# A hybrid attention block on one core: the last norm moved behind the first head's sigmoids, operands given out later, one more item split ahead, one output block reordered

## The chip, the cores and the metric

The kernel runs on one core of one Trainium2 chip. The metric is the device time of one execution in microseconds (us); the time of a kernel is the median of several executions.

## The reference

512 tokens and 16 meta tokens in front of them (528 positions) with 1024 features pass a layer norm and one wide projection. Two attention branches read it, their gated outputs are merged, projected once more, added to the normed input and normed again:

```
h    = layer_norm(concat(meta, x))
proj = h @ w_in                      # 10240 columns: q,k,v,gate of both branches, two merge gates
y_d  = rms_norm((softmax(q1 k1) - lam * softmax(q2 k2)) @ v) * 0.8        # 8 heads, width 128
y_s  = stick_breaking(q, k) @ v                                           # 16 heads, width 64
br_d = (y_d * silu(g_d)) @ w_br_diff ;  br_s = (y_s * silu(g_s)) @ w_br_sb
out  = layer_norm(2**0.25 * h + (sigmoid(m_d + b) * br_d + sigmoid(m_s + b) * br_s) @ w_out)
```

The stick-breaking weights are `sigmoid(z)` times a running product of `sigmoid(-z)`, so this branch needs sigmoids on ScalarE where the first branch needs exponentials, and the rms norm of a softmax head needs a logarithm and an exponential.

## The kernel before

All products run in float32 as three passes (high times high, high times low, low times high). So every weight tile is split before use: ScalarE casts it to `wh` (`hi`, line 153), VectorE subtracts to get `wl` (`lo`, line 158). One such tile of 128 x 512 is an **item**; 212 of them pass through 6 buffers each of `wh` and `wl`. `prep(h)` splits item `h`, and the projections call it for the item four further on (`AHEAD = 4`); it also calls `fetch`, which issues the next weight loads on SyncE's queue, and whatever was put on the list `later` for that many calls of `prep`.

The work has four parts.

- **Start**: layer norm, transposes, the first queries and keys; its order on each engine is as written.
- **Attention**: 16 units, first eight softmax heads ("d"), then eight pairs of stick-breaking heads ("s"). `run` (a loop over the projections of the next unit) hands out the current unit's steps at fixed points of a clock that counts projection work: scores, transposes of the attention weights (`transposed`: copies `ah` on ScalarE at line 625, remainders `al` on VectorE at line 626), products with the values (`d_values`, `s_values`, the latter at lines 774 to 783 into the one bank `av`). In this part the compiler's scheduler decides the final order on each engine, from a simulated time line. A softmax head's norm (`d_norm`: `ms` product at lines 735 and 736, Ln at 738, Exp at 739, VectorE's product at 741 that frees the bank `av`) is handed out 3.0 into the next unit, for the last head (7) 1.0. `s_scores` takes two sigmoids of each score bank (lines 760 and 762), then VectorE's scan (764) and product (765). There are two score banks (`psc`). Line 761 ties every sigmoid behind the newest Exp of a norm, so that ScalarE loads the table of the sigmoids once.
- **Merge and branch products**: order as written. Seven merge gates (`md` 3 to 7, `ms` 0 and 1) are projected while `operands(ydT)` forms the seven operand combinations `gh`, `gl` of the first branch in four parts (lines 850 to 857), given out at 0.3 and then every 7.5. Each branch product is four pairs of column blocks with seven products each (`pair`, line 875; copies of intermediate sums at 880, 882 and 884), a fast scheme that saves one product in eight. The `late` pool that holds `gh`, `gl` and their temporaries lies where the attention's buffers were, so its first writer waits for the last reader of those.
- **Output**: the gated sums are cast to `mh` (line 916) and `ml` (919), `w_out` is split to `wo0h`, `wo0l`, `wo1h`, `wo1l` (lines 936 and 937), and eight groups of 24 products (lines 993 to 995) run over four row blocks and two column halves. In the meantime SyncE loads the residual's parts (`eg`, `eb`, `hr`) and the rest of `w_out`; VectorE forms residual (966, 967), sum (1002), statistics (1005) and the final norm (1015, 1019).

Of the kernel before, what the change touches and what calls it, by code (L numbers as in the profile page):

```python
# [16 lines left out]
P = 128  # L17
D = 1024
KT = D // P
# [24 lines left out]
def hybrid_block_kernel(ctx: ExitStack, tc: tile.TileContext, x, meta, emb_g, emb_b, w_in, b_gate,  # L44
                        diff_lambda, subln_g, w_br_d, w_br_s, w_out, ln_g, ln_b, out):
    nc = tc.nc
    v, s, g, pe = nc.vector, nc.scalar, nc.gpsimd, nc.tensor
# [36 lines left out]
    for n, (kind, i) in enumerate(seq):  # L84
        if kind in ("BD", "BS"):
            w = w_br_d if kind == "BD" else w_br_s
# [21 lines left out]
    raw0 = ypool.tile([P, 4, KT, P], F32, tag="ys", name="raw0")  # L108
    raws, split, sums, later = {}, [], {}, []
    rings = {False: ("raw", 6, []), True: ("rawa", 4, [])}  # L110
    state = {"l": 0, "h": 0, "n": 0}
    pools = {False: wpool}

    def first_load(n):
# [44 lines left out]
        if isinstance(items[h], int):  # L159
            left[items[h]] -= 1  # L160

    AHEAD = 4

    def prep(h):

        state["n"] += 1
# [15 lines left out]
    def follow(ins, other):  # L182
        tc.add_manual_dep(ins, other.name, mybir.DependencyInfo(mybir.DependencyClass.NoSync, mybir.DependencyReason.DATA),
                          reason="order")

    def keep_order(first, engines=ORDERED):

# [249 lines left out]
    def proj_tok(res, kind, i):  # L437
        n = take(kind, i)
        ps = pj.tile([P, 512], F32, tag="pj", name="ps")
        for k in range(KT):  # L440
            if k % 4 == 0:
                prep(n + k // 4 + AHEAD)
            _, wh, wl = split[n + k // 4]
            pe.matmul(ps, wh[:, k % 4, :], hTh[:, k, M:], start=(k == 0), stop=False)  # L444
            pe.matmul(ps, wh[:, k % 4, :], hTl[:, k, M:], start=False, stop=False)  # L445
            pe.matmul(ps, wl[:, k % 4, :], hTh[:, k, M:], start=False, stop=(k == KT - 1))  # L446
            if k < KT - 1:
                yield 0.64
        res.append(ps)

    def proj_pos(res, kind, i):
        n = take(kind, i)
        for c in range(2):
            ps = pj.tile([P, 512], F32, tag="pj", name="ps")
            if n > 4:
                prep(n + c + AHEAD)
            for k in range(KT):
                _, wh, wl = split[n + k // 4]
                for m, (a, b) in enumerate(((wh, hTh), (wh, hTl), (wl, hTh))):
                    pe.matmul(ps[:, :H2], a[:, k % 4, :], b[:, k, ts(c, H2)], start=(k == 0 and m == 0),  # L460
                              stop=(k == KT - 1 and m == 2))
                if k < KT - 1:
                    yield 0.33
            res.append(ps)
            if c == 0:
                yield 0.33
# [34 lines left out]
    with tc.tile_pool(name="att", bufs=1) as ap:  # L501
# [230 lines left out]
        def d_norm(unit, h):  # L732
            av, sq = unit["av"], unit["sq"]
            ms = ptp.tile([P, 512], F32, tag="tp", name="ms")
            pe.matmul(ms, onesm, sq[0], start=True, stop=False)
            pe.matmul(ms, onesm, sq[1], start=False, stop=True)
            r = ap.tile([P, S], F32, tag="sq", name="r")
            s.activation(r, ms, AF.Ln, bias=epsr)
            s.activation(r, r, AF.Exp, scale=-0.5)
            state["exp"] = nc.cur_bb.bb.instructions[-1]  # L740
            v.scalar_tensor_tensor(ydT[:, h, :], av, g08, r, op0=ALU.mult, op1=ALU.mult)


        def s_scores(unit, c):
            K = unit["K"]
            A = unit["A"]
            a = apads[c]
            sg = ap.tile([P, ZW], F32, tag="e0", name="sgm", bufs=2)
            om = ap.tile([P, ZW], F32, tag="e1", name="om", bufs=2)
            for i in reversed(range(NB)):  # L750
                nk, z0 = NKEY[i], ZOFF[i]
                for n, (ps, k0, use, lo) in enumerate(logits(A[c], K[c], i)):
                    if n == 1:
                        yield
                    if k0 + use == nk:
                        w = P if lo is None else use
                        v.tensor_tensor(ps[:, use - w:use], ps[:, use - w:use], with_lo(lo, neg[:, M + P - w:], om[:, ds(z0, w)]),  # L757
                                        op=ALU.add)
                    o = ds(z0 + k0, use)
                    s.activation(om[:, o], ps[:, :use], AF.Sigmoid, scale=-1.0)  # L760
                    follow(nc.cur_bb.bb.instructions[-1], state["exp"])
                    s.activation(sg[:, o], ps[:, :use], AF.Sigmoid)
                rev = om[:, z0:z0 + nk][:, ::-1]
                v.tensor_tensor_scan(rev, rev, rev, 1.0, ALU.mult, ALU.min)  # L764
                v.tensor_tensor(a[:, ds(AOFF[i], nk - 1)], sg[:, ds(z0, nk - 1)], om[:, ds(z0 + 1, nk - 1)],
                                op=ALU.mult)
                yield
# [20 lines left out]
        def spread(gen, t0, dt, count):  # L788
            return [(t0 + dt * m, lambda: next(gen)) for m in range(count)]
# [12 lines left out]
        for u, (kind, n) in enumerate(UNITS):  # L802
            unit = units[u]
            last = u + 1 == len(UNITS)
            proj = [] if last else keys_values(units[u + 1], *UNITS[u + 1])
            if u + 2 < len(UNITS):
                proj.append(stage_q(units[u + 2], *UNITS[u + 2]))
            steps = pending + [(0.6, lambda unit=unit: values(unit, kind))]
            pending = []
            if kind == "d":  # L810
                ta = {}
                steps += spread(d_scores(unit, n), 0.0, TD[0], 10)
                parts = transposed(ta, apads[n % 2], "d")
                steps += [(TD[1] + 0.7 * m, f) for m, f in enumerate(parts)]
                steps.append((TD[2], lambda: d_values(unit, ta)))
                pending = [(3.0 if n < 7 else 1.0, lambda unit=unit, n=n: d_norm(unit, n))]
            else:
                if n == 0:
                    for a in apads:
                        for i in range(NB):  # L820
                            g.memset(a[:, ds(AOFF[i] + NKEY[i] - 1, 1)], 0.0)
                if last:
                    proj += [gate("d", n, ydT), merge_gate(0, 0), merge_gate(0, 1), merge_gate(0, 2), gate("s", n, ysT)]
                else:
                    proj += [gate("d", n, ydT), gate("s", n, ysT)]
                for c in range(2):
                    ta = {}
                    steps += spread(s_scores(unit, c), 4.4 * c + (2.0 if n == 0 and c == 0 else 0.0), 0.85, 5)
                    parts = transposed(ta, apads[c], c)
                    steps += [(7.0 + 6.5 * c + 0.7 * m, f) for m, f in enumerate(parts)]  # L830
                    steps.append((10.5 + 6.5 * c, lambda c=c, ta=ta: s_values(unit, c, n, ta)))
            run(proj, steps)
# [28 lines left out]
    def pair(kind, p, G, t, done):  # L861
# [6 lines left out]
        u, z7, w = c11, c22, c21 = [tmp[:, n, :] for n in range(3)]  # L868

        def product(q, bank, n, start=True):  # L870
            prep(h + q + AHEAD)
            _, wh, wl = split[h + q]
            for k in range(4):
                for m, (a, b) in enumerate(((wh, gh), (wh, gl), (wl, gh))):
                    pe.matmul(bank, a[:, k, :], b[:, n, k, :], start=start and k == 0 and m == 0, stop=k == 3 and m == 2,  # L875
                              skip_group_check=not start)
                yield 0.35
# [22 lines left out]
    G, parts = operands(ydT)  # L900
    early_ms = [gpool.tile([P, S], F32, tag="sg", name="sm1") for j in range(2)]
    run([merge_gate(0, j, MD[j]) for j in range(3, 8)] + [merge_gate(1, j, early_ms[j]) for j in range(2)],
        [(0.3 + 7.5 * i, f) for i, f in enumerate(parts)])
    for p in range(4):
        run([pair("BD", p, G, MD[2 * p:2 * p + 2], lambda m: None)])
    ss = ypool.tile([P, KT, S], F32, tag="yd", name="ss")
# [25 lines left out]
    def split_out(c, k):  # L932
# [5 lines left out]
        left[l] -= 1  # L938
        fetch()

    for p in range(4):
        steps = []
        if p == 3:
            run([merge_gate(1, 7, MS[7])])
            WO = [[hpool.tile([P, KT, 512], F32R, tag=f"hT{x}", name=f"wo0{x}") for x in "hl"]]
            steps = [(0.8 + 1.6 * k, lambda k=k: split_out(0, k)) for k in range(5)]
        run([pair("BS", p, G, MS[2 * p:2 * p + 2], lambda m, p=p: merged(2 * p + m))], steps)
# [36 lines left out]
    for c in range(2):  # L984
        for t in range(NB):
            st, final = sts[t], t == NB - 1
            for o, w in [(0, 256), (256, 256)] if final and c else [(0, 512)]:
                r, hr = ds(o, w), hrs[t][c]
                ps = pj.tile([P, 512], F32, tag="pj", name="pso")[:, :w]
                for n, k in enumerate((0, 1, 2, 3, 4, 5, 7, 6)):  # L990
                    mh, ml = MH[k][:, ts(t, P)], ML[:, k, ts(t, P)]
                    wh, wl = WO[c][0][:, k, r], WO[c][1][:, k, r]
                    pe.matmul(ps, mh, wh, start=(n == 0), stop=False)
                    pe.matmul(ps, mh, wl, start=False, stop=False)
                    pe.matmul(ps, ml, wh, start=False, stop=(n == KT - 1))
                if o == 0:
                    for work in MEANWHILE[NB * c + t]:
                        work()
# [63 lines left out]
```

## Time and profile before

| what | value |
|---|---|
| median of 3 runs | 737.57 us (736.24 to 739.0) |
| the profiled execution | 738.3 us |
| its span, first to last instruction | 736.5 us |
| TensorE busy, share of the span | 721.0 us, 98% |
| VectorE busy | 579.1 us, 79% |
| ScalarE busy | 445.3 us, 60% |
| mean granted TensorE clock | 0.993 |
| DMA | 71.84 MB, 98 GB/s on average |

The profiled execution lies 0.7 us above the median, and 1.8 us of it are outside the span. Line numbers are those of the kernel before; in the changed kernel the same lines stand 6 to 16 further down. "PE" is TensorE's matmul, "ACT" ScalarE, "DVE" VectorE, "POOL" GpSimd, "SPq" SyncE's queue. A matmul's duration is longer than the step from its start to the next one's start, since matmuls are pipelined: what a stall costs is read from the starts.

### The profile page before, as it was taken

Reading aid. Unit: us, or ns where it says so; the run is one execution under the profiler, and the core shown is the slowest. Engines: PE = TensorE matmul, PEld = TensorE weight load, DVE = VectorE, ACT = ScalarE, POOL = GpSimd, SP = SyncE. Lnnn points to the kernel's source line nnn. Section 1 sums busy time; section 2 is a strip of 40 time slices with the busy share of each in tenths; the row PEclk is TensorE's granted clock in tenths of the full one; section 3 lists DMA queues with packets and bytes.
Section 4 is the critical chain, followed back from the end, with each engine's and each line's share of the span. In section 5 each row is a group of like instructions: output and inputs, shape, how many; then the busy total and the mean of one; then the engine's idle time right before and its main releaser. Section 6 shows DMA issues by size and latency. Waiting matters only on the chain.

```text
span 736.5 us, 13070 instructions
## 1 busy us (share of the span) xinstructions
PE 721.0 (98%) x4658; PEld 658.0 (89%) x4658; DVE 579.1 (79%) x1304; ACT 445.3 (60%) x1099; POOL 90.2 (12%) x116
## 2 busy tenths in 40 slices
PE   8999999999999999999999999999999999999994
PEld 8999999999999897898989898988878998999784
DVE  6788778878876599696969696978486878788887
ACT  5686777777876667475757575756355456555300
POOL 3310110011000000100000000001002202230002
PEclk9999999999999999999999999999999999999997
DMA  9143221222122222213131222132129937696802
GB/s 280 48 115 87 58 75 46 83 58 87 52 65 72 79 79 58 58 44 100 44 92 54 85 73 76 54 86 67 49 75 196 186 101 186 133 184 183 314 17 101
DMA packets 121347, 71.84 MB, mean 98 GB/s; under 512 B 4241, under 2 KB 114994, under 8 KB 121282
## 3 DMA queue, kind: packets, MB, share of 16 engines
q1 hardware_dynamic: 111650, 64.18, 29.5%
q0 software_dynamic: 9312, 5.77, 6.0%
q10 hardware_dynamic: 320, 1.06, 0.4%
q8 instruction: 37, 0.61, 0.3%
q14 instruction: 28, 0.23, 0.1%
HBM read 67.32 MB, written 2.10 MB: 94 GB/s over the span
## 4 chain that ended last, share of the span: by engine, by line
PE 85%; DVE 8%; DMA 3%; issue 1%; ACT 1%; POOL 1%; SPq 0%; DVEq 0%; POOLq 0%; ACTq 0%
PE ps L460 23%; PE ps L444 11%; PE ps L446 11%; PE ps L445 11%; PE q L875 10%; PE sc L602 4%; PE t L615 3%; DMA raw<-in_w_out_dram 2%; PE t L620 1%; PE bank L335 1%; PE av L778 1%; PE tv L565 1%; PE av L779 1%; DMA eb<-in_emb_ln_b_dram 1%; DVE hr L1019 1%
## 5 line engine op out<-in xcount | busy, mean ns | idle before, releaser
L158 DVE TENSOR_TENSOR wl<-raw,wh 128x512 fp32r<-128x512 f32 x180 | 125.3, 703 | 44.7 <-ACT wh L153 43.3
L460 PE MATMUL ps<-hTh,wh 128*128 128x264 f32 x512 | 147.2, 287 | 0.0
L460 PE MATMUL ps<-hTl,wh 128*128 128x264 f32 x512 | 146.4, 286 | 0.0
L444 PE MATMUL ps<-hTh,wh 128*128 128x512 f32 x368 | 145.5, 395 | 0.6 <-ACT wh L153 0.6
L460 PE MATMUL ps<-hTh,wl 128*128 128x264 f32 x512 | 146.0, 285 | 0.0
L446 PE MATMUL ps<-hTh,wl 128*128 128x512 f32 x368 | 144.9, 394 | 0.6 <-DVE wl L158 0.6
L445 PE MATMUL ps<-hTl,wh 128*128 128x512 f32 x368 | 145.1, 394 | 0.0
L153 ACT CAST wh<-raw 128x512 fp32r<-128x512 f32 x180 | 110.2, 620 | 49.1 <-PE ps L445 38.3
L460 PEld LDWEIGHTS ps<-hTh,wh 128*128 128x128 f32 x512 | 96.4, 188 | 1.3
L460 PEld LDWEIGHTS ps<-hTl,wh 128*128 128x128 f32 x512 | 96.4, 188 | 0.9
L460 PEld LDWEIGHTS ps<-hTh,wl 128*128 128x128 f32 x512 | 96.4, 188 | 0.3
L446 PEld LDWEIGHTS ps<-hTh,wl 128*128 128x128 f32 x368 | 69.5, 189 | 14.7 <-DVE wl L158 1.1
L444 PEld LDWEIGHTS ps<-hTh,wh 128*128 128x128 f32 x368 | 69.5, 189 | 14.5 <-ACT wh L153 1.0
L445 PEld LDWEIGHTS ps<-hTl,wh 128*128 128x128 f32 x368 | 69.6, 189 | 13.0
L875 PE MATMUL q<-gh,wh 128*128 128x256 f32 x224 | 63.5, 284 | 0.2 <-ACT t L884 0.2
L875 PE MATMUL q<-gl,wh 128*128 128x256 f32 x224 | 63.4, 283 | 0.0
L875 PE MATMUL q<-gh,wl 128*128 128x256 f32 x224 | 63.4, 283 | 0.0
L626 DVE TENSOR_TENSOR al<-t,ah 128x512 fp32r<-128x512 f32 (+2 forms) x88 | 45.9, 526 | 19.9 <-ACT ah L625 13.4
L764 DVE TENSOR_TENSOR_SCAN om<-om 128x528 f32<-128x528 f32 (+2 forms) x64 | 55.0, 868 | 6.8 <-ACT om L760 6.4
L625 ACT CAST ah<-t 128x512 fp32r<-128x512 f32 (+2 forms) x88 | 39.9, 462 | 28.8 <-PE t L615 23.2
L602 PE MATMUL sc<-k,A 128*128 128x264 f32 (+2 forms) x256 | 56.5, 308 | 0.2 <-POOL k L519 0.2
L760 ACT ACTIVATE om<-sc 128x264 f32<-128x264 f32 (+3 forms) x80 | 31.7, 396 | 24.7 <-DVE sc L757 23.1
(242 smaller groups left out, 1437.4 us busy)
## 6 DMA issues: line engine op xcount, KB each, us to landing
raw<-in_w_in_dram SPq DMA_DIRECT2D x152, 256.0 KB, 3.0
raw<-in_w_out_dram SPq DMA_DIRECT2D x16, 256.0 KB, 3.8
raw<-in_w_br_diff_dram SPq DMA_DIRECT2D x12, 256.0 KB, 4.1
raw<-in_w_br_sb_dram SPq DMA_DIRECT2D x12, 256.0 KB, 4.3
raw<-in_w_in_dram SPq DMA_DIRECT2D x4, 512.0 KB, 6.5
rawa<-in_w_br_diff_dram SPq DMA_DIRECT2D x8, 256.0 KB, 5.2
rawa<-in_w_br_diff_dram POOLq DMA_DIRECT2D x8, 256.0 KB, 6.1
rawa<-in_w_br_sb_dram SPq DMA_DIRECT2D x8, 256.0 KB, 3.9
```

The lines of the kernel that those rows point to most:

```text
L153: s.copy(wh, raw)
L158: eng.tensor_tensor(wl, raw, wh.bitcast(F32), op=ALU.subtract)
L444: pe.matmul(ps, wh[:, k % 4, :], hTh[:, k, M:], start=(k == 0), stop=False)
L445: pe.matmul(ps, wh[:, k % 4, :], hTl[:, k, M:], start=False, stop=False)
L446: pe.matmul(ps, wl[:, k % 4, :], hTh[:, k, M:], start=False, stop=(k == KT - 1))
L460: pe.matmul(ps[:, :H2], a[:, k % 4, :], b[:, k, ts(c, H2)], start=(k == 0 and m == 0), stop=(k == KT - 1 and m == 2))
L602: pe.matmul(ps[:, :n], q, K[:, m, k0:k0 + n], start=(m == 0), stop=(m == 1))
L625: s.copy(h, t[:, o:o + w])
L626: v.tensor_tensor(l, t[:, o:o + w], h.bitcast(F32), op=ALU.subtract)
L760: s.activation(om[:, o], ps[:, :use], AF.Sigmoid, scale=-1.0)
L764: v.tensor_tensor_scan(rev, rev, rev, 1.0, ALU.mult, ALU.min)
L875: pe.matmul(bank, a[:, k, :], b[:, n, k, :], start=start and k == 0 and m == 0, stop=k == 3 and m == 2, skip_group_check=not start)
```

## The change

Four edits.

1. **Norm of head 7**: handed out at 5.8 of the first stick-breaking unit in place of 1.0; that unit's first head gives out its scores from 2.0 on (as before), the second from 6.3 in place of 4.4. ScalarE's order is tied in one chain for this unit only (`behind`): sigmoids of the first head, a load of the table that holds Ln and Exp, Ln, Exp, sigmoids of the second head. The tie of all other sigmoids behind an Exp is gone.
2. **Operands of the first branch** are given out at 3.5, 11.0, 18.5 and 26.0 in place of 0.3, 7.8, 15.3 and 22.8.
3. **`further`**: at 4.4 of the last merge gate, `prep` is called once more and the lead grows from four items to five for the last pair of branch products.
4. **First output block**: of its 24 products the three that read the low parts `wo0l` of blocks 5, 7 and 6 come last.

```
+    def behind(name, on=True):
+        if on:
+            ins = nc.cur_bb.bb.instructions[-1]
+            if name in state:
+                follow(ins, state[name])
+            state[name] = ins
...
+            if h == 7:
+                s.preload_act_table_set("natural_log_exp_and_others")
+                behind("act")
             s.activation(r, ms, AF.Ln, bias=epsr)
+            behind("act", h == 7)
             s.activation(r, r, AF.Exp, scale=-0.5)
-            state["exp"] = nc.cur_bb.bb.instructions[-1]
+            behind("act", h == 7)
...
                     s.activation(om[:, o], ps[:, :use], AF.Sigmoid, scale=-1.0)
-                    follow(nc.cur_bb.bb.instructions[-1], state["exp"])
+                    behind("act", first)
                     s.activation(sg[:, o], ps[:, :use], AF.Sigmoid)
+                    behind("act", first)
...
-                pending = [(3.0 if n < 7 else 1.0, lambda unit=unit, n=n: d_norm(unit, n))]
+                pending = [(3.0 if n < 7 else 5.8, lambda unit=unit, n=n: d_norm(unit, n))]
...
-                    steps += spread(s_scores(unit, c), 4.4 * c + (2.0 if n == 0 and c == 0 else 0.0), 0.85, 5)
+                    steps += spread(s_scores(unit, c, n == 0), (2.0 + 4.3 * c) if n == 0 else 4.4 * c, 0.85, 5)
...
-        [(0.3 + 7.5 * i, f) for i, f in enumerate(parts)])
+        [(3.5 + 7.5 * i, f) for i, f in enumerate(parts)])
...
+    def further():
+
+        state["ahead"] += 1
+        prep(len(split))
...
-            run([merge_gate(1, 7, MS[7])])
+            run([merge_gate(1, 7, MS[7])], [(4.4, further)])
...
+                products = [(k, m) for k in (0, 1, 2, 3, 4, 5, 7, 6) for m in ("hh", "hl", "lh")]
+                if t == 0 and c == 0:
+                    products.sort(key=lambda x: x[0] >= 5 and x[1] == "hl")
```

How the rows move. **First place**: ScalarE in the first stick-breaking unit, before. `r` is the norm of head 7 (Ln, then Exp), `om` and `sgm` the two sigmoids of a score bank, `wh` a weight item.

```order
L153 CAST wh<-raw 128x512 x2
L557 COPY vT<-ps 128x264
L153 CAST wh<-raw 128x512
L738 ACTIVATE r<-ms,epsr 128x512
L739 ACTIVATE r<-r 128x512
L760 ACT_TABLE_LOAD
L760 ACTIVATE om<-sc 128x264
L762 ACTIVATE sgm<-sc 128x264
L760 ACTIVATE om<-sc 128x264
L762 ACTIVATE sgm<-sc 128x264
```

The changed kernel's rows around the same norm; `om` and `sgm` ahead of the first load are the last sigmoids of the unit's first head, those behind the second load the first of its second head.

```order
L770 ACTIVATE om<-sc 128x144
L772 ACTIVATE sgm<-sc 128x144
L745 ACT_TABLE_LOAD
L153 CAST wh<-raw 128x512 x2
L563 COPY vT<-ps 128x264
L747 ACTIVATE r<-ms,epsr 128x512
L153 CAST wh<-raw 128x512
L749 ACTIVATE r<-r 128x512
L770 ACT_TABLE_LOAD
L770 ACTIVATE om<-sc 128x264
L772 ACTIVATE sgm<-sc 128x264
```

All of the first head's sigmoids now stand ahead of the norm, with a table load of their own, 34 rows ahead of the norm's; ScalarE loads a table three times here in place of once. From here to the end of the attention the scheduler gives a different order on TensorE, VectorE and ScalarE; the order on GpSimd and SyncE is unchanged in the whole program.

**Second place**: ScalarE where the attention ends and the first operand part begins, before. `half` is the last copy of the attention, `gh` the operand casts of part 0, `td` a merge gate's sigmoid.

```order
L473 ACTIVATE sg<-ps 128x512
L625 CAST ah_6710<-t_6704 128x288
L625 CAST ah_6714<-t_6704 128x160
L782 COPY half<-av 64x512
L856 CAST gh<-ydT 128x256
L856 CAST gh<-ydT 128x2x256
L856 CAST gh<-t 128x4x256
L153 CAST wh<-raw 128x512
L485 ACTIVATE td<-ps,cols 128x512
L153 CAST wh<-raw 128x512 x2
```

The same place in the changed kernel.

```order
L153 CAST wh<-raw 128x512
L479 ACTIVATE sg<-ps 128x512
L649 CAST a_451<-t_6688 16x32
L631 CAST ah_6711<-t_6705 128x288
L631 CAST ah_6715<-t_6705 128x160
L793 COPY half<-av 64x512
L867 CAST gh<-ydT 128x256
L867 CAST gh<-ydT 128x2x256
L867 CAST gh<-t 128x4x256
L491 ACTIVATE td<-ps,cols 128x512
L153 CAST wh<-raw 128x512 x2
```

One weight item that stood behind the operand part's three casts now stands six rows ahead of them; the same holds for its `wl` on VectorE.

**Third place**: ScalarE at the start of the last pair of branch products, before. `ss` is the last merge gate's sigmoid, `t` the three copies of intermediate sums, `wo0h` the casts of `w_out`.

```order
L153 CAST wh<-raw 128x512
L485 ACTIVATE ss<-ps,cols 128x512
L153 CAST wh<-rawa 128x512
L936 CAST wo0h<-raw 128x512
L880 COPY t<-q 128x256
L153 CAST wh<-raw 128x512
L936 CAST wo0h<-raw 128x512
L882 COPY t<-q 128x256
L153 CAST wh<-sum 128x512
L916 CAST mh<-ss 128x512
L936 CAST wo0h<-raw 128x512
L884 COPY t<-q 128x256
```

The same place in the changed kernel.

```order
L153 CAST wh<-rawa 128x512
L491 ACTIVATE ss<-ps,cols 128x512
L153 CAST wh<-raw 128x512
L947 CAST wo0h<-raw 128x512
L891 COPY t<-q 128x256
L153 CAST wh<-sum 128x512
L927 CAST mh<-ss 128x512
L947 CAST wo0h<-raw 128x512
L893 COPY t<-q 128x256
L927 CAST mh<-ss 128x512
L947 CAST wo0h<-raw 128x512
L895 COPY t<-q 128x256
```

Each of the last three items stands one product earlier, the first of them ahead of the gate's sigmoid, and the casts `mh` of the pair before follow one product earlier too; between the sigmoid and the third copy stand as many casts as before.

More of the change, by code (lines that the diff above doesn't have):

```diff
@@ L110, in hybrid_block_kernel @@
     rings = {False: ("raw", 6, []), True: ("rawa", 4, [])}
-    state = {"l": 0, "h": 0, "n": 0}
+    state = {"l": 0, "h": 0, "n": 0, "ahead": 4}
     pools = {False: wpool}
@@ L160, in lo @@
             left[items[h]] -= 1
-    AHEAD = 4
     def prep(h):
@@ L441, in proj_tok @@
             if k % 4 == 0:
-                prep(n + k // 4 + AHEAD)
+                prep(n + k // 4 + state["ahead"])
             _, wh, wl = split[n + k // 4]
@@ L455, in proj_pos @@
             if n > 4:
-                prep(n + c + AHEAD)
+                prep(n + c + state["ahead"])
             for k in range(KT):
@@ L737, in d_norm, with s_scores @@
             r = ap.tile([P, S], F32, tag="sq", name="r")
+            if h == 7:
+                s.preload_act_table_set("natural_log_exp_and_others")
+                behind("act")
             s.activation(r, ms, AF.Ln, bias=epsr)
+            behind("act", h == 7)
             s.activation(r, r, AF.Exp, scale=-0.5)
-            state["exp"] = nc.cur_bb.bb.instructions[-1]
+            behind("act", h == 7)
             v.scalar_tensor_tensor(ydT[:, h, :], av, g08, r, op0=ALU.mult, op1=ALU.mult)
-        def s_scores(unit, c):
+        def s_scores(unit, c, first):
             K = unit["K"]
@@ L870, in product @@
         def product(q, bank, n, start=True):
-            prep(h + q + AHEAD)
+            prep(h + q + state["ahead"])
             _, wh, wl = split[h + q]
@@ L989, in hybrid_block_kernel @@
                 ps = pj.tile([P, 512], F32, tag="pj", name="pso")[:, :w]
[L990 to L995, printed above, removed]
+                products = [(k, m) for k in (0, 1, 2, 3, 4, 5, 7, 6) for m in ("hh", "hl", "lh")]
+                if t == 0 and c == 0:
+                    products.sort(key=lambda x: x[0] >= 5 and x[1] == "hl")
+                for n, (k, (m, w)) in enumerate(products):
+                    pe.matmul(ps, MH[k][:, ts(t, P)] if m == "h" else ML[:, k, ts(t, P)], WO[c]["hl".index(w)][:, k, r],
+                              start=(n == 0), stop=(n == 3 * KT - 1))
                 if o == 0:
```

## Prediction

> **What bounds the kernel now.** I read the page first: busy times and the chain of work that ended last.
>
> ```profile
> PE 721.0 (98%) x4658; PEld 658.0 (89%) x4658; DVE 579.1 (79%) x1304; ACT 445.3 (60%) x1099; POOL 90.2 (12%) x116
> PE 85%; DVE 8%; DMA 3%; issue 1%; ACT 1%; POOL 1%; SPq 0%; DVEq 0%; POOLq 0%; ACTq 0%
> ```
>
> TensorE is the bound: busy for 98% of the span, and 85% of the last chain is its own work. No edit removes a product, so all that can be won on it is idle time and slow clock, and both are few. The waits of TensorE (us in total, times, longest) name them:
>
> ```profile
> PE av L779 <- DVE al L626: 1.3, 2, 1.1
> PE ps L444 <- ACT wh L153: 0.6, 1, 0.6
> PE ps L446 <- DVE wl L158: 0.6, 1, 0.6
> PE pso L994 <- DVE wo0l L937: 0.6, 2, 0.3
> ...
> PE q L875 <- ACT t L884: 0.2, 1, 0.2
> ```
>
> Each edit aims at one of these: the norm at the first, the operands at the next two, the output block at the fourth, the lead of five items at the fifth. What a wait costs I take from TensorE's starts, since its products overlap.
>
> **Edit 1, the norm behind the first head's sigmoids.** VectorE and ScalarE in the first stick-breaking unit, in order of time:
>
> ```profile
> 233.26 0.29 DVE L757 TENSOR_TENSOR sc<-sc,neg 128x128 f32<-128x128 f32 x1
> ...
> 248.33 0.69 ACT L738 ACTIVATE r<-ms,epsr 128x512 f32<-128x512 f32 x1
> 249.05 0.63 ACT L739 ACTIVATE r<-r 128x512 f32<-128x512 f32 x1
> 249.70 1.28 ACT L760 ACT_TABLE_LOAD   x1
> 251.00 0.39 ACT L760 ACTIVATE om<-sc 128x264 f32<-128x264 f32 x1
> ```
>
> The first score is masked at 233.26, but its sigmoid stands behind the norm and starts at 251.00. For nearly 18 us both score banks are held and the unit stands still; after that ScalarE and VectorE work off two heads and the next unit at once, until TensorE runs into the backlog. There are its starts in that unit's second head, then the same chain in a head without a wait:
>
> ```profile
> 289.26 0.30 PE L778 MATMUL av<-ah,V 128*128 128x288 f32 x1
> ...
> 291.75 0.43 PE L780 MATMUL av<-al,V 128*128 128x512 f32 x1
> ```
>
> ```profile
> 521.54 0.30 PE L778 MATMUL av<-ah,V 128*128 128x288 f32 x1
> ...
> 522.29 0.44 PE L780 MATMUL av<-al,V 128*128 128x512 f32 x1
> ```
>
> The stretch takes 2.49 us here and 0.75 us there: the wait costs 1.74 us (a little more, as the quick stretch also holds three transposes). Right behind it the clock is halved (us, TensorE busy and products, granted clock, DMA share, GB/s):
>
> ```profile
> 292.00:293.00 1.00, 1.00 (x5) 0.61 0.00 0
> 293.00:294.00 1.00, 1.00 (x4) 0.50 0.00 0
> 294.00:295.00 1.00, 1.00 (x4) 0.50 0.00 0
> 295.00:296.00 1.00, 1.00 (x4) 0.69 0.00 0
> ```
>
> The missing clock adds up to 0.39 + 0.50 + 0.50 + 0.31 = 1.70 us. Nowhere else between the start and the tail is the clock down, so I put this to the wait, and the term is 1.74 + 1.70 = 3.4 us.
>
> The Trainium skill states another rule (TensorE: Matmul & The Clock Gate, Part 1: The HAM clock gate): the clock is halved only after an idle window of about 3.4 us. The trace speaks against it here, with a longest wait of 1.1 us ahead of the halved clock; it is kept as a rival.
>
> What the edit adds: two table loads, 2 x 1.28 = 2.6 us of ScalarE. The first stands where the first sigmoid formerly waited, and 34 rows lie between it and the norm's. The danger is behind the norm. From its second `ms` product ScalarE does Ln 0.69, one cast, Exp 0.63, a load 1.28 and two sigmoids of 0.39 before the first score bank of the second head is free; with the cast at 0.61 (row below) that is 4.0 us at most. In the new order TensorE has 22 projection products in between, at a step of 0.22 us (next fence) 4.8 us, and nine transposes more. So the norm is hidden with 0.8 us and the transposes to spare; if that cover were gone, up to the two loads' 2.6 us come back. The bank `av` is freed by VectorE's product behind Exp, and asked for later still. I take zero.
>
> The Trainium skill speaks against the edit: group activations by table set, and a switch costs 1.28 us plus 1.38 us of drain, 2.66 us in all (ScalarE: Activation LUTs, Table sets: the hidden batching unit and What ACT_TABLE_LOAD costs). With its figure the chain behind the norm would be 5.4 us, an estimate, and hidden only by the transposes. The trace shows no drain: Exp, load and sigmoid follow each other within 0.04 us.
>
> **Edit 2, operands later.** TensorE, ScalarE and VectorE at the second and third wait:
>
> ```profile
> 540.77 0.39 PE L445 MATMUL ps<-hTl,wh 128*128 128x512 f32 x1
> 540.99 0.39 PE L446 MATMUL ps<-hTh,wl 128*128 128x512 f32 x1
> 542.00 0.50 PE L444 MATMUL ps<-hTh,wh 128*128 128x512 f32 x1 [0.62 <-ACT wh L153]
> ...
> 543.35 0.50 PE L446 MATMUL ps<-hTh,wl 128*128 128x512 f32 x1 [0.62 <-DVE wl L158]
> 543.68 0.39 PE L444 MATMUL ps<-hTh,wh 128*128 128x512 f32 x1
> ```
>
> ```profile
> 541.34 0.61 ACT L153 CAST wh<-raw 128x512 fp32r<-128x512 f32 x1
> ```
>
> ```profile
> 542.61 1.89 DVE L158 TENSOR_TENSOR wl<-raw,wh 128x512 fp32r<-128x512 f32 x3
> ```
>
> Four steps take 543.68 - 540.99 = 2.69 us where 0.88 would do: 1.8 us lost, at full clock. The item that TensorE asks for is split only behind the operand part, which itself stood waiting for the attention's buffers. In the new order this item stands ahead of the part, on both engines. What is late next is the item behind it: its `wl` is the first of the three in the last row, ready at 542.61 + 0.63 = 543.2; TensorE asks for it 15 steps behind 540.99, at 544.3. So 1.1 us remain, and the term is 1.8 us, with a floor of 0.7 if these two meet.
>
> The later parts each move behind one to two more items of 0.63 us on VectorE. Their cover is the time up to the branch products, in the timeline and the chain:
>
> ```profile
> 558.09 1.23 DVE L857 TENSOR_TENSOR gl<-t,gh 128x1024 fp32r<-128x1024 f32 x1 [0.19 <-ACT gh L856]
> ```
>
> ```profile
> 567.68 40.31 PE q L875 x336
> ```
>
> The last operand is there 8.4 us before; 1.8 us of shift and 1.3 us of items leave 5.3 us. Nothing.
>
> **Edits 3 and 4, the last pair and the output.** First, what sets the end there, in the chain that ended last:
>
> ```profile
> 688.00 6.49 DMA raw<-in_w_out_dram
> 695.25 5.66 DMA raw<-in_w_out_dram
> 700.93 0.62 ACT wo1h L936
> ```
>
> From the end of the branch products the chain is loads, then casts, then VectorE to the end; TensorE is not in it. Its last product starts at 726.37 and VectorE reads that sum at 728.66:
>
> ```profile
> 726.37 0.28 PE L995 MATMUL pso<-wo1h,ml 128*128 128x256 f32 x1
> ```
>
> ```profile
> 728.66 0.40 DVE L1002 SCALAR_TENSOR_TENSOR hr<-hr,pso 128x256 f32<-128x256 f32 x1
> ```
>
> So TensorE has about 2 us to spare at the end, and the 0.6 us of the output block's waits, if edit 4 ends them, only add to it: zero. But loads and VectorE's tail are set off by the end of the branch products, so what edits 1 and 2 win arrives whole.
>
> Edit 3 moves three splits one product ahead. The first of them, on VectorE:
>
> ```profile
> 672.18 0.69 DVE L158 TENSOR_TENSOR wl<-rawa,wh 128x512 fp32r<-128x512 f32 x1 [3.09 <-ACT wh L153]
> ```
>
> It stood behind the gate's sigmoid and moves into the 3.09 us of idle time ahead of it, so VectorE has 0.69 us less between there and the casts of `w_out` whose buffers the loads wait for. That may bring the loads forward by anything between zero and 0.69 us; I take 0.4, nearer to the moved row, since VectorE is full there. The wait on the third copy (0.2 us) stays: as many casts stand between the sigmoid and that copy as before. SyncE's and GpSimd's orders are the same, so no queue is passed.
>
> **The sum.** 3.4 + 1.8 + 0 + 0.4 = 5.6 us. The profiled execution would go from 738.3 to 732.7; it lay 0.7 above the median, so the median goes from 737.57 to **732.0 us**.
>
> **The rivals.**
>
> - *One new wait in the re-ordered attention.* From the norm on the scheduler has put the steps of eight units elsewhere, and each bank and each `al` copy is a place for a wait; the likeliest is the score bank behind the norm, with the two loads. For it: only 0.8 us and the transposes cover the norm. Against: such a wait occurs once in the old order, behind an 18 us backlog that is now gone. Price between 1.7 us (a wait like the old one) and 3.4 us (with the clock): 733.7 to 735.4. Two such: up to 738.8, no change.
> - *The clock falls without the wait.* If the slow stretch has another cause, 1.70 us stay: 733.7. For it speaks the skill's rule named above; against it that the clock falls nowhere else.
> - *TensorE sets the end after all.* Then edit 4's 0.6 us and edit 3's 0.2 us count in full: 731.2. Against: the 2 us above.
> - *Slower: the wait recurs.* If without the tie behind the norm the next units' sigmoids come as close on each other's heels as the old backlog did, `av` waits for `al` at the end of every head, each at 3.4 us with the clock. From the second on the 5.6 us are spent; three give 742.2. Seven units with two heads each offer the place. Against: the old order had these units too, with no wait of TensorE on them but the one.
> - *The change does not do what it says.* The rows of the new order show that it does.
>
> **How the numbers follow.** A measurement of this kernel can tell about 0.5% from no change, 3.7 us: faster is below 733.9, slower above 741.3. Forecast 0.55, whose own range is 730.5 to 733.4 (the transposes and the two waits won as well, against the floor of edit 2, and 0.3 of scatter, the three runs lying between 736.24 and 739.0). TensorE at the end 0.07, clock 0.05, one new wait 0.25 (0.05 of it still below 733.9), two 0.03, slower 0.05. Faster: 0.55 + 0.07 + 0.05 + 0.05 = 0.72. Same: 0.20 + 0.03 = 0.23. Slower 0.05. The range runs from 730.2, below the third rival, to 735.4, the dear end of the first, and leaves out the two-wait and slower cases and the tails of the forecast.
>
> **What would show it.** Right: no wait of TensorE on `al`, `wh` or `wl` among its waits; clock 1.00 from 40 us to the last products; three table loads, the first near 233; the loads of `w_out` in the chain's end 5 to 6 us earlier than 688.0 and 695.3, and behind them still casts and VectorE. Edit 4 is wrong as costed if TensorE's wait on `wo0l` is gone and the last sum is read directly behind its product. The forecast is wrong if a score or an `av` product has a wait above 1 us with a clock near 0.5 behind it, or if the branch products start 5 us earlier and the end does not.

## The result and the profile after

| | before | after |
|---|---|---|
| median | 737.28 us (736.24 to 739.0, 6 runs) | 732.11 us (731.66 to 732.59, 6 runs) |
| the profiled execution, its span | 738.3 us, 736.5 us | 732.59 us, 730.8 us |
| mean granted TensorE clock there | 0.993 | 0.995 |

The ratio of after to before is 0.993, 95% interval 0.9917 to 0.9943: faster by 0.7%, beyond the 0.5% that the prediction takes as the least that can be told from no change. The forecast was 732.0. A copy of the changed kernel in a later group gave 732.2 (731.35 to 732.49, 6 runs).

The page of after, busy times and shares of the last chain:

```profile
PE 718.3 (98%) x4658; PEld 657.6 (90%) x4658; DVE 580.3 (79%) x1304; ACT 447.2 (61%) x1101; POOL 89.9 (12%) x116
PE 89%; DVE 5%; DMA 3%; POOL 1%; ACT 1%; issue 1%; SPq 0%; POOLq 0%; DVEq 0%; ACTq 0%
```

TensorE has the same 4658 products in 2.7 us less busy time. The halved clock in the attention, which is gone, accounts for 1.7 us of this; the same changed kernel differs by 1.1 us from one profiled execution to the next (718.3 here, 717.2 in the later copy). TensorE's share of the last chain grows from 85% to 89%, and VectorE's falls from 8% to 5%. All TensorE's waits in after:

```profile
PE warm L271 <- POOL idents masks.py:199: 1.4, 1, 1.4
PE sc L608 <- POOL k L525: 0.2, 1, 0.2
PE q L886 <- ACT t L895: 0.2, 1, 0.2
```

Those on `al`, `wh`, `wl` and `wo0l` are gone; the third copy's 0.2 us stays. To see where the time came from, four starts on TensorE cut the span into pieces: first and last product of the attention, first branch product, first output product. Before, then after:

```profile
65.07 0.40 PE L714 MATMUL av<-ah,V 128*128 128x512 f32 x1
535.70 0.43 PE L780 MATMUL av<-al,V 128*128 128x512 f32 x1
567.51 0.28 PE L875 MATMUL q<-gh,wh 128*128 128x256 f32 x1
681.33 0.40 PE L993 MATMUL pso<-wo0h,mh 128*128 128x512 f32 x1
```

```profile
65.10 0.40 PE L720 MATMUL av<-ah,V 128*128 128x512 f32 x1
531.96 0.44 PE L791 MATMUL av<-al,V 128*128 128x512 f32 x1
562.17 0.28 PE L886 MATMUL q<-gh,wh 128*128 128x256 f32 x1
675.93 0.40 PE L1010 MATMUL pso<-wo0h,mh 128*128 128x512 f32 x1
```

The attention (first row to second) takes 470.63 before and 466.86 after, 3.77 less. From there to the branch products it is 31.81 and 30.21, 1.60 less; the branch products take 113.82 and 113.76. The whole span shrinks by 5.7, so the output part gives the last 0.3. ScalarE around the moved norm, in order of time:

```profile
232.46 1.28 ACT L770 ACT_TABLE_LOAD   x1
233.76 0.39 ACT L770 ACTIVATE om<-sc 128x264 f32<-128x264 f32 x1
...
247.53 1.28 ACT L745 ACT_TABLE_LOAD   x1
...
250.14 0.69 ACT L747 ACTIVATE r<-ms,epsr 128x512 f32<-128x512 f32 x1
...
251.23 0.64 ACT L749 ACTIVATE r<-r 128x512 f32<-128x512 f32 x1
251.89 1.28 ACT L770 ACT_TABLE_LOAD   x1
253.19 0.39 ACT L770 ACTIVATE om<-sc 128x264 f32<-128x264 f32 x1
253.47 0.38 ACT L772 ACTIVATE sgm<-sc 128x264 f32<-128x264 f32 x1
```

The first sigmoid starts at 233.76, 17 us earlier than 251.00, and there are three loads in place of one. The second head's first score bank is read out at 253.47 + 0.38 = 253.85, and TensorE writes the next scores at 254.67, 0.8 us later, without a wait:

```profile
254.67 0.53 PE L608 MATMUL sc<-k,A 128*128 128x400 f32 x2
```

At the operands, the item next in line, on VectorE (the first of these two) and on TensorE:

```profile
538.86 1.29 DVE L158 TENSOR_TENSOR wl<-raw,wh 128x512 fp32r<-128x512 f32 x2
```

```profile
540.87 0.39 PE L452 MATMUL ps<-hTh,wl 128*128 128x512 f32 x1
```

Its `wl` is ready at 538.86 + 0.69 = 539.55, 1.3 us early. The end, in the chain that ended last and in the last sum on the two engines:

```profile
675.94 5.85 DMA eb<-in_emb_ln_b_dram
681.86 6.62 DMA raw<-in_w_out_dram
688.54 0.67 DVE wo1l L948
689.21 5.96 DMA raw<-in_w_out_dram
```

```profile
719.94 0.28 PE L1010 MATMUL pso<-wo1h,ml 128*128 128x256 f32 x1
```

```profile
722.94 0.40 DVE L1018 SCALAR_TENSOR_TENSOR hr<-hr,pso 128x256 f32<-128x256 f32 x1
```

The loads of `w_out` come 6.1 and 6.0 us earlier than 688.00 and 695.25, VectorE still ends the kernel, and TensorE has 3.0 us to spare where it had 2.3.

### The profile page after: what moved, and what is told of

Same layout as the page of the kernel before. It is cut to its first block, busy times and chain, and to the rows that moved or that the text cites. A ratio compares the mean times of both kernels' runs of the same rounds, so it can differ in the third digit from the quotient of the medians.

```text
span 730.8 us, 13070 instructions
## 1 busy us (share of the span) xinstructions
PE 718.3 (98%) x4658; PEld 657.6 (90%) x4658; DVE 580.3 (79%) x1304; ACT 447.2 (61%) x1101; POOL 89.9 (12%) x116
## 4 chain that ended last, share of the span: by engine, by line
PE 89%; DVE 5%; DMA 3%; POOL 1%; ACT 1%; issue 1%; SPq 0%; POOLq 0%; DVEq 0%; ACTq 0%
PE ps L466 25%; PE ps L450 12%; PE ps L451 12%; PE ps L452 12%; PE q L886 10%; PE sc L608 5%; PE t L621 4%; DMA raw<-in_w_out_dram 2%; PE t L626 1%; PE bank L341 1%; PE av L789 1%; PE tv L571 1%; PE av L790 1%; DMA eb<-in_emb_ln_b_dram 1%; DVE hr L1035 1%
## 5 line engine op out<-in xcount | busy, mean ns | idle before, releaser
L775 DVE TENSOR_TENSOR_SCAN om<-om 128x528 f32<-128x528 f32 (+1 forms) x64 | 55.7, 877 | 5.1 <-ACT om L770 4.4
```

## The experiments

Twelve runs in three groups; before was run again beside each group: 737.49 (23 runs), 737.15 (11) and 737.28 (11). The first four hold one edit each, the next four all but one, and the last four begin with the changed kernel itself. With them stand the pieces of their traces, cut at the four starts as above (attention, operands, branch products).

**One edit alone: the norm.** Before, with the lines of edit 1 only, of which the core is

```
-                pending = [(3.0 if n < 7 else 1.0, lambda unit=unit, n=n: d_norm(unit, n))]
+                pending = [(3.0 if n < 7 else 5.8, lambda unit=unit, n=n: d_norm(unit, n))]
```

> The kernel before with edit 1 alone (norm of head 7 behind the first head's sigmoids). Theory (a wait of TensorE on al and the halved clock behind it are both due to the 18 us backlog): 3.4 to 3.6 us less than before, clock 1.00 through the attention, the two waits at the first operand part still there at 0.6 us each. Rival (the clock falls without the wait): 1.7 to 1.9 us less, with a stretch of clock 0.5 still between 280 and 300 us. Rival (edits help each other): less than 3 us, with the rest appearing only when all four are made.

Measured 734.44 us (733.47 to 734.83, 6 runs), ratio 0.9955 (0.9941 to 0.9968). Pieces 466.80, 31.79, 113.80: the attention alone is shorter, by 3.8. The next waits are still there:

```profile
PE ps L454 <- DVE wl L158: 0.6, 1, 0.6
...
PE ps L452 <- ACT wh L153: 0.4, 1, 0.4
```

None on `al` is left, so that wait belongs to edit 1 and to nothing else in the change. Edit 1 has three parts (the later norm, the later scores of the second head, the dropped tie of all other sigmoids); no run holds one of them alone, so which of them it takes is not shown. The gain of the medians, 3.05, is less than the trace's 3.8; the next run shows why.

**One edit alone: the operands.**

```
-        [(0.3 + 7.5 * i, f) for i, f in enumerate(parts)])
+        [(3.5 + 7.5 * i, f) for i, f in enumerate(parts)])
```

> The kernel before with edit 2 alone (operand parts given out 3.2 later). Theory: 1.8 us less than before, no wait of TensorE on wh or wl, the 1.1 us wait on al and the slow clock behind it as before. Rival (the wait moves to the next item): 0 to 0.7 us less, with a wait on the item behind it.

Measured 735.04 us (734.2 to 735.77, 6 runs), ratio 0.9963 (0.9949 to 0.9977), 2.45 us by the medians where 1.8 were expected. Pieces 469.15, 30.00, 113.80. The operands' piece is 1.81 shorter, just the expected term. But the attention is 1.48 shorter too, and the edit touches nothing there. The wait is the same:

```profile
PE av L779 <- DVE al L626: 1.3, 2, 1.1
```

The clock is not. TensorE around this wait in this kernel (us; busy time and instructions of TensorE, its weight loads, VectorE, ScalarE and GpSimd; granted clock; DMA share, GB/s):

```profile
290.00:291.00 1.00, 0.67 (x2) 0.37 (x2) 0.94 (x4) 0.50 (x2) 0.00 (x0) 1.00 0.11 33
291.00:292.00 1.00, 0.10 (x1) 0.10 (x1) 0.97 (x4) 0.98 (x3) 0.00 (x0) 1.00 0.79 221
292.00:293.00 1.00, 1.00 (x5) 0.71 (x6) 0.97 (x2) 0.98 (x4) 0.00 (x0) 1.00 0.03 8
```

TensorE is idle as long as before, and no halved clock follows. What the prediction put to the wait as a fixed price is paid only in some executions.

**One edit alone: the lead.**

```
-            run([merge_gate(1, 7, MS[7])])
+            run([merge_gate(1, 7, MS[7])], [(4.4, further)])
```

> The kernel before with edit 3 alone (one more item split ahead for the last pair). Theory (the tail is set by loads and VectorE, and the moved split lets the casts of w_out and so the loads come earlier): 0.3 to 0.4 us less, TensorE's wait on the third copy still 0.2 us. Rival (TensorE sets the end): 0 us, or 0.2 us if that wait goes; VectorE's last sum read directly behind TensorE's last product.

Measured 737.44 us (735.37 to 738.02, 12 runs), ratio 0.9992 (0.9982 to 1.0003). The interval holds the expected 0.4 us and zero alike: before itself scatters over nearly 4 us. Pieces 470.55, 31.81, 113.76; this profiled execution had the halved clock.

**One edit alone: the output block.**

```
+                if t == 0 and c == 0:
+                    products.sort(key=lambda x: x[0] >= 5 and x[1] == "hl")
```

> The kernel before with edit 4 alone (three low products of the first output block last). Theory (TensorE has 2 us to spare at the end): no change, within 0.2 us, though TensorE's last product comes 0.5 to 1.3 us earlier. Rival (TensorE sets the end): 0.6 to 1.3 us less.

Measured 737.83 us (735.62 to 738.65, 12 runs), ratio 1.0 (0.9988 to 1.0012). Pieces 469.16, 31.81, 113.81: this profiled execution also had the whole wait and no halved clock. TensorE's last product starts 44.52 us behind its first output product, where it was 45.04 before, and the time does not follow.

**All but the norm.**

```
-                pending = [(3.0 if n < 7 else 5.8, lambda unit=unit, n=n: d_norm(unit, n))]
+                pending = [(3.0 if n < 7 else 1.0, lambda unit=unit, n=n: d_norm(unit, n))]
```

> The changed kernel without its first edit: the norm of head 7 stands ahead of the first head's sigmoids again, and the wait of av on al comes back (1.1 us in the trace). By the sum on record this gives back 3.4 us: 735.5. Theory A, formed after the first four runs: the wait itself costs about 2.0 us in every execution, and it sets off the halved clock (1.7 us more) only in about half of them: executions near 734.1 with a mean clock of 0.995 or more, and near 735.8 with 0.994 or less. Theory B: the halved clock needs the later waits on wh and wl as well, which are gone here: no execution at the low clock, median 734.1. The run with the operands' edit alone had the wait on al and no low clock in 6 executions, which by A is chance and by B the rule.

Measured 735.41 us (733.79 to 736.16, 7 runs), ratio to before 0.9973 (0.996 to 0.9985). Pieces 470.66, 30.00, 113.76. Here the clock behind the wait is halved, with no wait on `wh` or `wl` left:

```profile
290.00:291.00 1.00, 0.47 (x2) 0.19 (x1) 0.97 (x3) 0.58 (x2) 0.00 (x0) 1.00 0.26 71
291.00:292.00 1.00, 0.39 (x2) 0.33 (x3) 0.97 (x4) 0.98 (x4) 0.00 (x0) 1.00 0.64 191
292.00:293.00 1.00, 1.00 (x5) 0.81 (x4) 0.97 (x2) 0.97 (x4) 0.00 (x0) 0.54 0.00 0
293.00:294.00 1.00, 1.00 (x4) 0.81 (x3) 0.97 (x3) 0.94 (x5) 0.00 (x0) 0.50 0.00 0
294.00:295.00 1.00, 1.00 (x4) 0.81 (x3) 1.00 (x3) 0.57 (x2) 0.00 (x0) 0.50 0.00 0
295.00:296.00 1.00, 1.00 (x5) 0.74 (x5) 0.94 (x3) 0.00 (x0) 0.11 (x1) 0.75 0.00 0
```

The same wait as in the kernel with the operands alone, and 0.46 + 0.50 + 0.50 + 0.25 = 1.71 us of clock missing. Theory B falls. The runs are of two kinds, as theory A has it: 733.79 to 734.82 at clocks of 0.995 and 0.996, 735.85 to 736.16 at 0.992 to 0.994. The clock of 0.995 (735.41) in the profiled execution, which has the halved stretch, shows that the mean over a whole execution marks the kind only roughly: it also holds the half clock at the end of the span, which begins between 723 and 729 us in all the traces.

**All but the operands.**

```
-        [(3.5 + 7.5 * i, f) for i, f in enumerate(parts)])
+        [(0.3 + 7.5 * i, f) for i, f in enumerate(parts)])
```

> The changed kernel without its second edit: the waits on wh and wl of 0.6 us each come back. By the sum on record 1.8 us are given back: 733.9. By what the edit did alone, 2.5 us: 734.6. No low clock is expected, since the wait on al is gone.

Measured 734.3 us (733.03 to 735.12, 5 runs), ratio to before 0.9961 (0.9948 to 0.9974). Pieces 466.73, 31.85, 113.76. Beside after's 30.21 the operands' piece is 1.64 longer, and both waits are back. The sum's 733.9 is nearer than 734.6 by the pieces; by the medians both lie within the scatter.

**All but the lead.**

```
-            run([merge_gate(1, 7, MS[7])], [(4.4, further)])
+            run([merge_gate(1, 7, MS[7])])
```

> The changed kernel without its third edit (the split five items ahead in the last pair). By the sum on record 0.4 us are given back: 732.5, with the loads of w_out in the last chain that much later. Rival: the moved split costs nothing on the path, 732.1. The executions without the wait on al scatter by under 0.5 us, so that 0.4 us may be told apart here.

Measured 733.0 us (731.99 to 733.23, 5 runs), ratio to before 0.9941 (0.9929 to 0.9954); the whole change 732.2 and 732.11, so 0.8 to 0.9 by the medians where 0.4 were expected. The trace shows the step. SyncE's first load of the residual and VectorE's last three remainders of `wo0`, in this kernel and then in after:

```profile
677.04 1.92 SPq L975 DMA_DIRECT2D hr<-in_x_dram  x4
```

```profile
679.53 1.89 DVE L950 TENSOR_TENSOR wo0l<-raw,wo0h 128x512 fp32r<-128x512 f32 x3
```

```profile
676.47 1.80 SPq L978 DMA_DIRECT2D hr<-in_x_dram  x4
```

```profile
678.93 1.89 DVE L948 TENSOR_TENSOR wo0l<-raw,wo0h 128x512 fp32r<-128x512 f32 x3
```

At equal starts of the output (675.96 and 675.93) both come 0.57 and 0.60 us later without the edit: the moved row's own step, near the upper end (0.69) of what the prediction left open. The last chain of this kernel runs over other loads (`lgb` at 680.03 for 8.60 us), and its last load of `w_out` is issued at 689.55, 0.34 behind after's 689.21.

**All but the output block.**

```
-                if t == 0 and c == 0:
-                    products.sort(key=lambda x: x[0] >= 5 and x[1] == "hl")
```

> The changed kernel without its fourth edit (order of the products in the output's first block). By the sum on record nothing is given back, since the end is set by loads and VectorE: 732.1, with a wait of pso on wo0h or wo0l of 0.3 to 0.6 us in the trace. Rival, TensorE sets the end: 732.6.

Measured 732.2 us (731.53 to 732.79, 5 runs), the same as with it. TensorE's wait on `wo0l` was 0.2 us, a little under the expected 0.3 to 0.6, and its last product starts 44.49 us behind its first output product in place of after's 44.01. The rival, that TensorE sets the end, has nothing for it.

**The whole change again.** No edit.

> The changed kernel itself, beside the others of this group: 732.1 again, no execution at a mean clock of 0.993 or less. If edit 3 is worth what leaving it out gave back (0.4 to 0.9 us), this is that much below 732.7 to 733.0.

Measured 732.2 us (731.35 to 732.49, 6 runs), ratio 0.9922 (0.9905 to 0.9938). Pieces 466.71, 30.22, 113.75; clocks 0.994 to 0.996.

**Two more table loads behind the norm.** The changed kernel with

```
             s.activation(r, r, AF.Exp, scale=-0.5)
             behind("act", h == 7)
+            if h == 7:
+                for table in ("sigmoid_and_others", "natural_log_exp_and_others"):
+                    s.preload_act_table_set(table)
+                    behind("act")
```

> The changed kernel with two more table loads on ScalarE between the last norm and the second head's sigmoids (2 x 1.28 = 2.56 us; nothing else is added). The changed trace has the score bank free 0.9 us before TensorE asks for it. The sum on record, that the loads are hidden only with that margin, then gives a wait of sc of 1.6 to 1.7 us at about 255 and 733.8, and 735.3 where that wait halves the clock as well. Rival, the loads are hidden by more than the margin says, because the scheduler or later idle time of ScalarE gives way: no wait over 0.5 us and 732.1.

Measured 734.34 us (733.54 to 735.22, 6 runs), 2.1 above its neighbour. ScalarE, then TensorE's next scores and the wait that appeared:

```profile
251.71 2.57 ACT L753 ACT_TABLE_LOAD   x2
254.28 1.28 ACT L774 ACT_TABLE_LOAD   x1
255.58 0.39 ACT L774 ACTIVATE om<-sc 128x264 f32<-128x264 f32 x1
```

```profile
257.49 0.52 PE L608 MATMUL sc<-k,A 128*128 128x400 f32 x2
...
268.95 0.34 PE L794 MATMUL av<-al,V 128*128 128x160 f32 x1 [1.34 <-DVE al L632]
```

The sigmoid is 2.4 us later (255.58 against 253.19). The scores had been put later by the scheduler and did not wait; the delay came out in the first head's products with the values, as a wait on `al` of 1.34 us, and the attention's piece is 469.40, 2.7 longer. So the loads are not hidden by more than a margin: two more of them, 2.6 us, cost 2.1 us by the medians and 2.7 by the piece, at another place than expected. As the order changed with them, how much of the margin of 0.8 us was used up is not told apart. No execution of this kernel was below a clock of 0.995, though the wait is longer than the one at 291.

**A shorter wait.** The kernel with all but the norm, its last product put ahead of the one that waits, in the first unit's second head:

```
-                pe.matmul(o, V[c][:, j, :], ta[j][1], start=False, stop=False)
-            pe.matmul(av, V[c][:, 0, :], ta[0][1], start=False, stop=True)
+                if not (late and j == 3):
+                    pe.matmul(o, V[c][:, j, :], ta[j][1], start=False, stop=False)
+            pe.matmul(av, V[c][:, 0, :], ta[0][1], start=False, stop=not late)
+            if late:
+                pe.matmul(o, V[c][:, 3, :], ta[3][1], start=False, stop=True)
```

> The changed kernel without its first edit, and in the first unit's second head the last product of av is put ahead of the one that waits for al (the same sum in another order): the wait of 1.14 us becomes 0.92. Theory A, the clock is halved the more often the longer TensorE stands: clearly fewer executions with a mean clock of 0.993 or less than with the whole wait (before: 14 of 34), median 734.1. Theory C, any such wait halves the clock in about half of the executions, by chance of its place: median between 734.1 and 735.5 with both kinds, as without the edit.

```profile
291.96 0.34 PE L784 MATMUL av<-al,V 128*128 128x160 f32 x1 [0.87 <-DVE al L626]
```

Measured 734.84 us (733.82 to 735.69, 6 runs), with clocks of 0.992 (735.69) and 0.993 (735.18) in two runs of six; the profiled execution has no halved clock. Pieces 469.21, 30.00, 113.76: the attention was not shorter for it. Two of six beside 18 of 45 runs of before is no difference that six runs can show, so the counts do not tell theories A and C apart; the last section comes back to them.

**A longer wait, which failed.** The kernel with all but the operands, and

```
-        s.copy(wh, raw)
+        for m in range(3 if h == 135 else 1):
+            s.copy(wh, raw)
```

> The changed kernel without its second edit, with the cast of the one item that TensorE waits for made three times instead of once (2 x 0.53 us more on ScalarE, same values): the wait of ps on wh grows from 0.4 to about 1.5 us, and that on wl stays at 0.6. Wait alone: 734.2 + 1.1 = 735.3. Theory A, the clock is halved by the length of the wait: most executions have the halved clock behind it, 1.5 us more, 736.8. Theory C: about half of them, 735.3 to 736.8. Theory D, the halved clock belongs to the place at 292 us and not to waits as such: none, 735.3.

Measured 734.04 us (733.97 to 734.5, 6 runs), and the waits as without the edit:

```profile
PE ps L455 <- DVE wl L159: 0.6, 1, 0.6
PE ps L453 <- ACT wh L154: 0.4, 1, 0.4
```

The extra casts fell on another item, at 509 us, where ScalarE had room; the one that TensorE waits for is cast at 537.63. The wait did not grow, so this run says nothing on the clock.

## Why the prediction was right, and where not

**Edit 1, the wait (1.74 us expected): right in kind, too small.** The attention takes 470.55 to 470.66 where wait and halved clock both occur (before, the lead alone, all but the norm), 469.15 to 469.21 with the wait alone (operands alone, output block alone, shorter wait), and 466.70 to 466.86 in the seven traces with the norm moved and no extra loads. So the stretch that went with the backlog costs 2.4 us, 0.6 more than the two rows compared; "a little more" was said of three transposes. TensorE's idle time in the attention was 1.43 to 1.46 us in four of these traces (before, all but the norm, operands alone, output block alone), made up of 1.14, 0.2 and 0.1 between 275 and 292 us, and none in after. Where the remaining 0.9 us went is not shown.

**Edit 1, the clock (1.70 us expected): the mis-sized term.** Between the first two groups of traces lie 1.3 to 1.5 us, a little under the missing clock. But it is paid only in part of the executions. Before, 18 of 45 runs have a mean clock of 0.993 or less, at 738.6 us on average; the 25 at 0.995 or more average 736.7. Of the 39 runs without the wait (the changed kernel twice, five others) none is at 0.993 or less. The profiled execution of before was one with the halved clock, and the prediction took its 1.70 us off every execution. The rival "the clock falls without the wait" is wrong: in no trace without the wait does it fall in the attention. The Trainium skill (TensorE: Matmul & The Clock Gate, Part 1: The HAM clock gate) states that the gate looks at a free-running window of about 3.4 us. The halved stretches agree: 1.70 us missing at half clock is 3.4 us. Its condition, an idle window, does not as it stands: in the two microseconds ahead of the halved clock of the run with all but the norm TensorE was busy for 0.47 and 0.39 us. What sets off the half clock here, and why only in part of the executions, stands in the last section.

**Edit 1, the added loads: right.** No wait on a score bank, at a margin of 0.8 us. The working was off in the parts: Ln began 1.9 us after the second `ms` product at 248.28 and not at once, since casts stood ahead of it, and the transposes and scores in TensorE's order covered that. Two more loads cost 2.1 us. The Trainium skill's 1.38 us of drain per switch (ScalarE: Activation LUTs, What ACT_TABLE_LOAD costs) is not in any of these rows: in the run with more loads the sigmoid starts 0.02 us behind the third load.

**Edit 2 (1.8 us expected): right.** 1.81 alone, 1.64 beside the other edits, and the next item's margin was 1.3 where 1.1 had been worked out.

**Edit 3 (0.4 us expected, up to 0.69): right, nearer the upper end.** VectorE's row moved by 0.60 us; the last loads by 0.34. Over all traces, counted from the first output product, that row starts at 4.76 to 4.77 us in the five without the edit and at 4.20 to 4.22 in the nine with it; the whole output part takes 54.50 to 55.35 us (mean 55.05) and 53.95 to 55.12 (mean 54.57). So the step is sure, and its worth at the end, 0.5 us, is a mean of ranges that overlap. **Edit 4 (0): right.**

**The sum** was 5.6 and the profiled executions differ by 5.7: 3.8 + 1.6 + 0.06 + 0.3. For a typical execution it had two errors that partly cancel: 0.6 too little for the wait, and a clock term that should have been 18/45 of 1.5, so 0.6 in place of 1.7. With both mended the pieces give 2.4 + 0.6 + 1.6 + 0.06 + 0.3 = 5.0; the medians of 6 runs each differ by 5.2. That the forecast of 732.0 was met within 0.1 us is therefore in part luck. Against the runs of before at a clock of 0.995 or more (736.7) the gain to 732.1 is 4.6, against those at 0.993 or less (738.6) 6.5. The rivals of one new wait, of TensorE at the end and of recurring waits found nothing in the traces.

## What to carry to other kernels

Cut a span at a few starts that every variant has, and compare pieces: the first three agreed within 0.2 us among traces that should agree, where the interval of a ratio of medians was 1.5 us wide (the lead alone). It does not help everywhere: the output part, set by loads, scattered by over 1 us. A wait is worth more than its own row if a backlog feeds it, so compare the whole stretch with the same stretch elsewhere. A price that one profiled execution shows, a slow clock above all, is multiplied by how often the runs pay it before it goes into a median.

## What the runs showed of the hardware

**The clock.** Of the seven traces with a wait of 0.87 to 1.34 us inside the attention three have the halved clock (before, the lead alone, all but the norm), and each of these lost 1.70 to 1.71 us. The 1.14 us wait ended at 291.49, 291.57 and 291.61 in those three, and at 291.67 and 291.90 in the two that kept full clock. Waits of 0.4 and 0.6 us were never followed by it in the traces. The two runs that were to find out what decides did not; the kept traces say more.

The times at which the granted clock changes lie on a grid of 3.413 us in each of the 14 traces. Before has full clock from 5.50, half from 292.21, full from 295.63 and half from 729.12: 0, 84, 85 and 212 steps. The grid lies at another place in each execution (its first change comes at 4.55 to 7.57). Two windows of it in before (columns as in the run with the operands alone):

```profile
288.80:292.21 3.41, 2.06 (x12) 1.41 (x10) 3.32 (x8) 2.39 (x7) 0.00 (x0) 1.00 0.26 77
292.21:295.62 3.41, 3.41 (x10) 2.62 (x10) 3.32 (x7) 2.25 (x8) 0.00 (x0) 0.50 0.00 0
```

The half clock follows the window that holds the wait and the few products ahead of it. Busy time alone does not decide: it is 2.06 to 2.09 us in the three halved cases, and with 2.08 us the window around the wait of the run with two more loads kept full clock. The streamed columns do. As an estimate, a product of 512 columns is taken to stream for 0.22 us from its start, the step used in the prediction, and others in proportion; what falls into the window around the wait is added up:

| trace | window | columns | clock behind it |
|---|---|---|---|
| all but the norm | 288.66 to 292.08 | 2685 | half |
| before | 288.80 to 292.21 | 2768 | half |
| the lead alone | 288.43 to 291.84 | 2769 | half |
| a shorter wait | 288.66 to 292.07 | 3136 | full |
| output block alone | 290.02 to 293.43 | 3203 | full |
| two more loads | 266.83 to 270.25 | 3787 | full |
| operands alone | 287.85 to 291.27 | 3898 | full |

From 40 us to the end of the span, in all 14 traces, half clock follows every window of up to 2769 columns and none of 2984 or more; no window lies between. So the same wait halves the clock or not by where the borders of the grid fall. A window laid at any place over the two traces with the 1.14 us wait and full clock would hold fewer than 2800 to 3000 columns at 0.42 to 0.49 of the places; for the shorter wait it is 0.30 to 0.34, and for the wait of 1.34 us and the waits at the operands it is none, since more products stand around them. The measured shares of runs at a mean clock of 0.993 or less are 18 of 45 for before (33 of 82 with the four other kernels that have the whole wait), 2 of 6, 0 of 6 and 0 of 17. Theories A and C thus both hold in part: a shorter wait is hit less often, and each hit is a matter of place. All this was read from the traces afterwards; no run moved the grid on purpose.

Three table loads in a row took 1.28 to 1.29 us each, with no gap before the sigmoid.
